# A chunk's contribution to the SSD state: one product of fp32 operands, or three products of split operands

## The chip, the cores and the metric

The kernel runs on one core of a Trainium2 chip. The metric is the device time of one execution in microseconds (us); runs are summed up by their median. Engines are named as in the profile: PE (TensorE, matrix products), PEld (its weight loads), DVE (VectorE), ACT (ScalarE), POOL (GpSimd) and SP (SyncE, which here only issues transfers). `L1535` is line 1535 of the kernel.

## The reference

One step of a decoder layer: a pooling branch beside a Mamba-2 SSD branch, merged by sigmoid gates, for a prompt of 1024 rows and 8 short samples. What matters here is the SSD of the prompt. The prompt is cut into 8 chunks of 128 rows, the 32 heads (64 wide each) form 4 groups of 8, and the heads of a group share B and C (128 wide). The state `h` is carried from chunk to chunk:

```
def step(h, inp):
    xq, dq, Bq, Cq = inp
    acs = jnp.cumsum(dq * Ag, axis=1)
    seg = acs[:, :, None] - acs[:, None, :]
    decay = jnp.exp(jnp.where(mask, seg, -jnp.inf))
    cb = jnp.einsum('bign,bjgn->bijg', Cq, Bq)
    att = cb[..., None] * decay * dq[:, None]
    y = jnp.einsum('bijge,bjgep->bigep', att, xq)
    y = y + jnp.einsum('bign,bige,bgepn->bigep', Cq, jnp.exp(acs), h)
    last = acs[:, -1]
    w_in = jnp.exp(last[:, None] - acs) * dq
    h = h * jnp.exp(last)[..., None, None] + jnp.einsum('bjgn,bjge,bjgep->bgepn', Bq, w_in, xq)
    return h, y
```

The last sum, over the rows `j` of a chunk, is the product that the change touches: B turned (rows by state, 128x128) against x weighted by `w_in` (rows by 8 heads of 64, 128x512), once per group and chunk, 32 times in all.

## The kernel before

All inputs are fp32. The large products are computed from split operands: a value is copied by ScalarE into a rounded high half (type fp32r), the rest (value less high half) is computed by VectorE or POOL as a low half, and three fp32r products, high·high, high·low and low·high, add up in PSUM (`gemm_`, `L359` to `L361`, here 12 products a block, that is three for each of four slices of 128 rows of the sum). Smaller products take fp32 operands as they are.

The work goes in stages: the first products and the modulation, the input projection (up to about 820 us, with the samples' SSD beside it), the chunk stage (about 820 to 1104 us), and the output products.

In the chunk stage, `chunk(g, c)` is a generator with one instance for each group `g` and chunk `c`, listed in `seq`, and each `yield` ends a step of it:

- loads of the decays (`dec`, L1492), of B and C (`bc`) and of x (`xb`, L1497), on SP's queue;
- the exponentials on ScalarE (`cE` L1501, `exps` L1201) behind a masking on POOL (`far` L1192);
- the transposes of x into the PSUM buffer `px` (L1510) and of B into `pbc` (L1512), and C·B (L1513) into the same buffer; ScalarE copies B turned to `bt` (L1515) and, for `c > 0`, C into `pbc` (L1517); VectorE makes `xd` (x by dt, L1521) and `xw` (x by `wdT`, L1523), and multiplies `dec` (L1528) and `cE` (L1530) by what stands in `pbc`;
- the state's product `pu` (L1535, PSUM pool `pc`, one buffer), the chunk's output `pi` (`inner`, L1213 and L1216), the new state `hn` (POOL L1541, VectorE L1543, or ScalarE L1539 for `c == 0`), and D·x added to `pi` in `xb` (L1548);
- `finish`: the gating by z (VectorE L1468), the split of the result (ScalarE L1470, POOL L1472), and sums of squares (ScalarE L1471, POOL L1473 to L1479);
- behind a group's last chunk, the state turned back (L1555), copied to a tile `fo` with the tag of x (L1557), and stored.

`px`, `pbc` and `pi` come from one PSUM pool, `ps`, of four buffers (`PB`). Blocks of the output products (`products`, from P_unit and S_unit) are woven in; they use the pool `mm` of three buffers (`PA`), and ScalarE (L1741) or VectorE (L1744, L1723) empties them. Their weights (`whi`, `wlo`, L459 and L460) are requested two units ahead (a unit is three blocks), with four buffers each. A loop over `i` sets the order; for the order of PE and SP what it traces is binding (`in_line(order)`), while DVE, ACT and POOL follow the order that the framework's scheduler gives them. In turn `i` stand the transposes of chunk `i + 1`, blocks, the products of chunk `i`, the loads of chunk `i + 3`, the exponentials of chunk `i + 2`, the finish of chunk `i`, a step of splitting w_o (`wo_splits`, ScalarE L1778, from `i > 12`), and blocks. 2.56 blocks come to a turn, so one or two lie between the products of a chunk and the next transposes.

Of the kernel before, what the change touches and what calls it, by code (L numbers as in the profile page):

```python
# [8 lines left out]
F32 = mybir.dt.float32  # L9
F32R = mybir.dt.float32r  # L10
AF = mybir.ActivationFunctionType
ALU = mybir.AluOpType
# [8 lines left out]
P = 128  # L21
# [25 lines left out]
def tile_pool_ssd_step(  # L47
# [9 lines left out]
    def nm(s):  # L57
        uid[0] += 1
        return f"{s}_{uid[0]}"
# [34 lines left out]
    def Y4(pool, dt=F32R):  # L94
        return pool.tile([P, 4, T], dt, tag="Y", name=nm("Y"), bufs=2)

    def PB():
        return psB.tile([P, 512], F32, tag="ps", name=nm("ps"))
# [4 lines left out]
    def PC():  # L103

        return psC.tile([P, 512], F32, tag="pc", name=nm("pc"))
# [6 lines left out]
    mm = nc.tensor.matmul  # L112
    act = nc.scalar.activation
    V = nc.vector
# [1069 lines left out]
    def decays(dec, g, c):  # L1184

        S = P if c < NC else NS
        load(dec, acs_d[c, 8 * g:8 * g + 8, :S].partition_broadcast(S))

    def far(dec, c):

        if c < NC:
            nc.gpsimd.affine_select(dec, dec, [[0, 8], [1, P]], ALU.is_ge, FAR, base=0, channel_multiplier=-1)  # L1192
        else:
            dS = dec.rearrange("p h (b i) -> p h b i", i=8)
            nc.gpsimd.affine_select(dS, dS, [[0, 8], [8, NB], [1, 8]], ALU.is_ge, FAR, base=0, channel_multiplier=-1)
            nc.gpsimd.affine_select(dS, dS, [[0, 8], [-8, NB], [0, 8]], ALU.is_ge, FAR, base=0, channel_multiplier=1)

    def exps(dec, g, c):
        S = P if c < NC else NS
        for h in range(8):  # L1200
            act(dec[:, h], dec[:, h], AF.Exp, bias=acT[:S, c, 8 * g + h:8 * g + h + 1], scale=-1.0)  # L1201
# [6 lines left out]
    def inner(xd, dec, S, state=None, cE=None):  # L1208
        pi = PB()
        for q in range(4):  # L1210
            o = [pi[64 * hh:64 * hh + 64, q * S:(q + 1) * S] for hh in range(2)]
            for hh in range(2):
                mm(o[hh], xd[:S, 2 * q + hh, :], dec[:S, 2 * q + hh], start=True, stop=state is None)  # L1213
            for hh in range(2 if state is not None else 0):
                h = 2 * q + hh
                mm(o[hh], state[:, h * 64:h * 64 + 64], cE[:, h], start=False, stop=True)  # L1216
        return pi[:, :4 * S].rearrange("p (q i) -> p q i", i=S)
# [245 lines left out]
    def ckt(shape, tag, bufs=2):  # L1463
        return (cl if tag in CKL else ca if tag in ("dec", "xb", "cE", "bc") else ck).tile(list(shape), F32, tag=tag, name=nm(tag), bufs=bufs)

    def finish(g, o, S, v, sz):

        V.tensor_tensor(v, v, sz, ALU.mult)  # L1468
        yhc = yh[g][:, :, o:o + S]
        act(yhc, v, AF.Copy)  # L1470
        act(sz, v, AF.Square)  # L1471
        nc.gpsimd.tensor_tensor(yl[g][:, :, o:o + S], v, yhc.bitcast(F32), ALU.subtract)  # L1472
        nc.gpsimd.tensor_tensor(sz[:, 0:2], sz[:, 0:2], sz[:, 2:4], ALU.add)  # L1473
        sa = sq_acc[:, o:o + S]
        if g == 0:
            nc.gpsimd.tensor_tensor(sa, sz[:, 0], sz[:, 1], ALU.add)
        else:
            nc.gpsimd.tensor_tensor(sz[:, 0], sz[:, 0], sz[:, 1], ALU.add)
            nc.gpsimd.tensor_tensor(sa, sa, sz[:, 0], ALU.add)  # L1479

    def sample_end(g):
        sz = ckt([P, 4, NS], "szs", 1)
        load(sz, z_d[g][:, :, SEQ:])
        v = ckt([P, 4, NS], "v", 1)
        load(v, ys_d[g])
        yield
        finish(g, SEQ, NS, v, sz)

    def chunk(g, c):
        o = c * P  # L1490
        dec = ckt([P, 8, P], "dec", 3)
        decays(dec, g, c)  # L1492
        bc = ckt([P, 2, P], "bc", 3)
        load(bc, xbc_d[g][:, 4:6, o:o + P])
        Bf, Cf = bc[:, 0], bc[:, 1]
        xb = ckt([P, 4, P], "xb", 5)
        load(xb, xbc_d[g][:, 0:4, o:o + P])  # L1497
        yield
        if c > 0:
            cE = ckt([P, 8, P], "cE")  # L1500
            act(cE, dec, AF.Exp, scale=-1.0)  # L1501
        if g > 0 or c > 0:
            far(dec, c)
            exps(dec, g, c)
            yield
        sz = ckt([P, 4, P], "sz", 3)
        load(sz, z_d[g][:, :, o:o + P])
        px = PB()
        for q in range(4):
            nc.tensor.transpose(px[:, q * P:(q + 1) * P], xb[:, q], ident)  # L1510
        pbc = PB()
        nc.tensor.transpose(pbc[:, :P], Bf, ident)  # L1512
        mm(pbc[:, P:2 * P], Bf, Cf, start=True, stop=True)  # L1513
        bt = ckt([P, P], "bt", 2)
        act(bt, pbc[:, :P], AF.Copy)  # L1515
        if c > 0:
            act(pbc[:, 2 * P:3 * P], Cf, AF.Copy)  # L1517
        pxv = px.rearrange("p (h d) -> p h d", d=64)
        heads = slice(8 * g, 8 * g + 8)
        xd = ckt([P, 8, 64], "xd", 2)  # L1520
        V.tensor_tensor(xd, pxv, dtT[:, c, heads].unsqueeze(2).to_broadcast([P, 8, 64]), ALU.mult)  # L1521
        xw = ckt([P, 8, 64], "xw", 1)
        V.tensor_tensor(xw, pxv, wdT[:, c, heads].unsqueeze(2).to_broadcast([P, 8, 64]), ALU.mult)  # L1523
        if g == c == 0:
            yield
            far(dec, c)
            exps(dec, g, c)
        V.tensor_tensor(dec, dec, pbc[:, P:2 * P].unsqueeze(1).to_broadcast([P, 8, P]), ALU.mult)  # L1528
        if c > 0:
            V.tensor_tensor(cE, cE, pbc[:, 2 * P:3 * P].unsqueeze(1).to_broadcast([P, 8, P]), ALU.mult)  # L1530
        yield
        if c == 0:
            yh[g], yl[g] = [Y4(hs if g % 2 else hp) for _ in range(2)]
        pu = PC()
        mm(pu, bt, xw.rearrange("p h d -> p (h d)"), start=True, stop=True)  # L1535
        pi = inner(xd, dec, P, *((hst[g], cE) if c > 0 else ()))
        hn = ckt([P, 512], "hst", 2)
        if c == 0:
            act(hn, pu, AF.Copy)  # L1539
        else:  # L1540
            nc.gpsimd.tensor_tensor(hn.rearrange("p (h d) -> p h d", d=64), hst[g].rearrange("p (h d) -> p h d", d=64),  # L1541
                                    Elb[:, c, heads].unsqueeze(2).to_broadcast([P, 8, 64]), ALU.mult)
            V.tensor_tensor(hn, hn, pu, ALU.add)  # L1543
        hst[g] = hn

        v = xb
        for q in range(4):
            V.scalar_tensor_tensor(v[:, q], v[:, q], Dv[:, 4 * g + q:4 * g + q + 1], pi[:, q], ALU.mult, ALU.add)  # L1548
        yield
        finish(g, o, P, v, sz)  # L1550
        if c == NC - 1:
            yield
            pt = PB()
            for q in range(4):
                nc.tensor.transpose(pt[:, q * P:(q + 1) * P], hn[:, q * P:(q + 1) * P], ident)  # L1555
            fo = ckt([P, 4, P], "xb", 5)
            act(fo, pt.rearrange("p (q n) -> p q n", n=P), AF.Copy)  # L1557
            store_(new_ssm_p[0, 0, 8 * g:8 * g + 8].rearrange("(q h) p n -> (h p) q n", h=2), fo)

# [125 lines left out]
    def to_chunks():  # L1685
        nonlocal right, ca
        right.__exit__(None, None, None)
        right = tc.tile_pool(name="ca", bufs=3, side="right", reuse_waits="tile")
        ca = right.__enter__()
        right_all.append(right)  # L1690
        seq.extend(chunk(g, c) for g in range(NG) for c in range(NC))
        next(seq[0])
    first_ws, first_g = {}, []
    ca = None
    seq = []
# [14 lines left out]
    ck = right.__enter__()  # L1710
# [78 lines left out]
    def products(t):  # L1789

        nonlocal made
        while made < RATE * t:
            next(pc_, None)
            made += 1
# [5 lines left out]
    for _ in range(FRONT - 1):  # L1800
        next(pc_)
    next(seq[0])
    next(seq[1])
    next(pc_)
    in_line(first_engines)
    order = tuple(mybir.EngineType[e] for e in ORDER)
    for i in range(len(seq)):
        if i + 1 < len(seq):
            next(seq[i + 1])
        products(i + 0.4)  # L1810
        if i > 0:
            next(seq[i - 1], None)
        next(seq[i], None)
        if i % NC == 2:
            ends = sample_end(i // NC)
            next(ends)
        if i + 3 < len(seq):
            next(seq[i + 3])
        if i + 2 < len(seq):
            next(seq[i + 2])  # L1820
        next(seq[i], None)
        if i % NC == 4:
            next(ends, None)
        if i > 12:
            next(wos, None)
        products(i + 1.0)
# [127 lines left out]
    for half in range(2):  # L1954
        c = slice(half * 512, half * 512 + 512)
# [102 lines left out]
```

## Time and profile before

| | |
|---|---|
| median of 3 runs | 1286.67 us (1284.23 to 1289.22) |
| profiled execution, its own time | 1286.55 us |
| its span, first to last instruction | 1284.8 us |
| mean granted clock of TensorE | 0.998 |
| PE busy in the span | 1256.1 us, 98% |
| DVE, ACT, POOL busy | 897.6 us (70%), 662.2 us (52%), 670.9 us (52%) |
| `L1535`, the product of the change | 64 records, 831.2 to 1101.8 us |

The profile shows one execution. A row of a group of instructions has the line, engine, operation, output and inputs by tile names, shapes and count, then the busy time and the mean duration, then the engine's idle time in front of these instructions with what ended it. The chain of waits goes back from the last instruction, at each step to what released it, or to the instruction ahead of it on its engine; a step's length is the time for which it held that path. The end of a product is modelled, and one product overlaps the next, so spacing is read from starts or from the chain, not from durations. An fp32 product of this kind leaves two records, one of split operands a single record.

### The profile page before, as it was taken

What the parts mean: (1) busy time and instruction counts of PE and PEld (TensorE: products, weight loads), DVE (VectorE), ACT (ScalarE), POOL (GpSimd) and SP (SyncE); (2) the same over time, 40 slices, a digit from 0 to 9 for tenths busy, and PEclk for the clock granted to TensorE, in tenths of its full rate; (3) what the DMA queues carried; (4) which work ended last, traced back from release to release, by engine and by line L of the source; (5) the groups of instructions that cost most, each with busy time, mean ns of one, the idle gap of its engine ahead of it and who ended that gap; (6) DMA issues with size and microseconds to landing.
All of it is one profiled execution on the core that took longest, in us unless ns stands there. A gap on an engine that the chain in (4) does not pass through costs nothing.

```text
span 1284.8 us, 26305 instructions
## 1 busy us (share of the span) xinstructions
PE 1256.1 (98%) x9739; PEld 1169.3 (91%) x9739; DVE 897.6 (70%) x1608; ACT 662.2 (52%) x1528; POOL 670.9 (52%) x563
## 2 busy tenths in 40 slices
PE   7999999999999999999999999999999999999997
PEld 6779999989999999999999999989888889999786
DVE  4686678965978688676676765587766877576443
ACT  4665347465556556454655554656675766202111
POOL 1007669678868878555444444355665867314000
PEclk9999999999999999999999999999999999999999
DMA  9736355465456544444556564999769898675631
GB/s 331 243 118 215 122 164 156 149 199 173 148 161 207 159 152 131 166 154 122 176 170 198 165 191 143 336 307 314 225 215 277 265 294 265 211 265 162 229 107 49
DMA packets 232769, 251.68 MB, mean 196 GB/s; under 512 B 29729, under 2 KB 176881, under 8 KB 232634
## 3 DMA queue, kind: packets, MB, share of 16 engines
q1 hardware_dynamic: 160544, 171.60, 42.9%
q10 hardware_dynamic: 72098, 78.41, 17.9%
q8 instruction: 77, 1.26, 0.4%
q14 instruction: 50, 0.41, 0.1%
HBM read 167.06 MB, written 83.01 MB: 195 GB/s over the span
## 4 chain that ended last, share of the span: by engine, by line
PE 63%; issue 7%; DMA 7%; POOL 4%; ACT 2%; DVE 2%; SPq 0%; ACTq 0%; POOLq 0%; DVEq 0%
PE ps L608 6%; PE ps L609 5%; PE ps L610 5%; PE mm L608 5%; PE mm L610 5%; PE mm L609 5%; PE mm L359 4%; PE mm L360 4%; PE mm L361 4%; PE ps L1213 3%; PE ps L2004 2%; PE ps L2006 2%; PE ps L2005 2%; PE pc L1535 2%; PE ps L1216 2%
## 5 line engine op out<-in xcount | busy, mean ns | idle before, releaser
L168 POOL TENSOR_TENSOR wlo<-rawA,whi 128x512 fp32r<-128x512 f32 x120 | 179.6, 1501 | 176.1 <-ACT whi L165 99.8
L168 POOL TENSOR_TENSOR wlo<-raw,whi 128x512 fp32r<-128x512 f32 x92 | 150.6, 1644 | 125.5 <-ACT whi L165 114.1
L359 PE MATMUL mm<-Y,whi 128*128 128x352 f32 (+1 forms) x480 | 163.5, 341 | 0.6 <-DVE G L1907 0.5
L360 PE MATMUL mm<-Y,whi 128*128 128x352 f32 (+1 forms) x480 | 157.4, 328 | 0.3 <-DVE Y L1573 0.3
L361 PE MATMUL mm<-Y,wlo 128*128 128x352 f32 (+1 forms) x480 | 156.8, 327 | 0.0
L608 PE MATMUL mm<-Y,whi 128*128 128x272 f32 x496 | 146.3, 295 | 0.6 <-DVE GA L624 0.5
L610 PE MATMUL mm<-Y,wlo 128*128 128x272 f32 x496 | 144.2, 291 | 2.2 <-POOL wlo L168 1.7
L608 PE MATMUL ps<-Y,whi 128*128 128x272 f32 x496 | 143.4, 289 | 2.5 <-ACT o L808 2.2
L609 PE MATMUL ps<-Y,whi 128*128 128x272 f32 x496 | 143.0, 288 | 0.0
L610 PE MATMUL ps<-Y,wlo 128*128 128x272 f32 x496 | 142.6, 287 | 0.0
L609 PE MATMUL mm<-Y,whi 128*128 128x272 f32 x496 | 142.6, 288 | 0.0
L1056 DVE SCALAR_TENSOR_TENSOR GA<-GA,cvT,GA 128x1112 f32<-128x1112 f32 x72 | 127.7, 1776 | 1.3 <-ACT GA L1053 1.3
L165 ACT ACTIVATE whi<-rawA 128x512 fp32r<-128x512 f32 x125 | 78.3, 627 | 89.7 <-PE ps L609 48.0
L165 ACT ACTIVATE whi<-raw 128x512 fp32r<-128x512 f32 x96 | 58.9, 627 | 104.6 <-DVE raw L554 48.7
L1201 ACT ACTIVATE dec<-dec,acT 128x128 f32<-128x128 f32 (+1 forms) x288 | 86.6, 383 | 23.2 <-POOL dec L1192 22.8
L610 PEld LDWEIGHTS mm<-Y,wlo 128*128 128x128 f32 x496 | 93.4, 188 | 3.8 <-POOL wlo L168 2.6
L359 PEld LDWEIGHTS mm<-Y,whi 128*128 128x128 f32 x480 | 90.2, 188 | 7.1 <-issue 4.8
L608 PEld LDWEIGHTS ps<-Y,whi 128*128 128x128 f32 x496 | 93.3, 188 | 3.1 <-ACT o L808 2.5
L608 PEld LDWEIGHTS mm<-Y,whi 128*128 128x128 f32 x496 | 93.3, 188 | 3.0 <-DVE GA L624 0.6
L609 PEld LDWEIGHTS mm<-Y,whi 128*128 128x128 f32 x496 | 93.4, 188 | 0.9
L610 PEld LDWEIGHTS ps<-Y,wlo 128*128 128x128 f32 x496 | 93.4, 188 | 0.0
L609 PEld LDWEIGHTS ps<-Y,whi 128*128 128x128 f32 x496 | 93.3, 188 | 0.0
(456 smaller groups left out, 3760.4 us busy)
## 6 DMA issues: line engine op xcount, KB each, us to landing
rawA<-in_w_in SPq DMA_DIRECT2D x46, 512.0 KB
dec<-acs_d SPq DMA_DIRECT2D x32, 512.0 KB
xbc<-GA ACTq DMA_DIRECT2D x24, 512.0 KB
rawA<-in_w_in SPq DMA_DIRECT2D x32, 256.0 KB
pw<-in_w_ssm_out ACTq DMA_DIRECT2D x32, 256.0 KB
ws<-ph ACTq DMA_DIRECT2D x32, 256.0 KB
ws<-pw SPq DMA_DIRECT2D x32, 256.0 KB
h<-in_state_ssm SPq DMA_DIRECT2D x32, 256.0 KB
```

What stands on the lines that cost most here:

```text
L165: ins = act(hi[:, :, :ncols], raw[:, :, :ncols], AF.Copy)
L168: (eng or nc.gpsimd).tensor_tensor(lo[:, :, :ncols], raw[:, :, :ncols], hi[:, :, :ncols].bitcast(F32), ALU.subtract)
L359: mm(ps[:, :n], a, rh[k][:, o:o + n], start=(k == 0), stop=False)
L360: mm(ps[:, :n], a, rl[k][:, o:o + n], start=False, stop=False)
L361: mm(ps[:, :n], b, rh[k][:, o:o + n], start=False, stop=(k == nk - 1))
L608: mm(p, hi, ah, start=(k == 0), stop=False)
L609: mm(p, hi, al, start=False, stop=False)
L610: mm(p, lo, ah, start=False, stop=(k == 3))
L1056: V.scalar_tensor_tensor(d[:, :n], rp[:, k:k + n], cvT[:, 24 * k + mc:24 * k + mc + 1], d[:, :n], ALU.mult, ALU.add)
L1201: act(dec[:, h], dec[:, h], AF.Exp, bias=acT[:S, c, 8 * g + h:8 * g + h + 1], scale=-1.0)
L1213: mm(o[hh], xd[:S, 2 * q + hh, :], dec[:S, 2 * q + hh], start=True, stop=state is None)
L1216: mm(o[hh], state[:, h * 64:h * 64 + 64], cE[:, h], start=False, stop=True)
```

## The change

The product `pu` is made from split operands. x is weighted in place in PSUM (the output of L1523 is `pxv` itself), and a new step splits weighted x into `xwh` and `xwl` (512 wide) and B turned into `bth` and `btl` (128 wide): the high halves by ScalarE, the low ones by VectorE, both out of PSUM. Three products then add up in `pu`. The tile `xw` and the two buffers of `bt` give way to four tiles of one buffer each, and the tile tag of x has four buffers instead of five. The loop gets one call more in each turn, so that the split of chunk `i + 1` is traced behind the products of chunk `i`; the opening gets one for chunk 0.

```
-        xb = ckt([P, 4, P], "xb", 5)
+        xb = ckt([P, 4, P], "xb", 4)
...
         pbc = PB()
         nc.tensor.transpose(pbc[:, :P], Bf, ident)
         mm(pbc[:, P:2 * P], Bf, Cf, start=True, stop=True)
-        bt = ckt([P, P], "bt", 2)
-        act(bt, pbc[:, :P], AF.Copy)
         if c > 0:
             act(pbc[:, 2 * P:3 * P], Cf, AF.Copy)
...
         V.tensor_tensor(xd, pxv, dtT[:, c, heads].unsqueeze(2).to_broadcast([P, 8, 64]), ALU.mult)
-        xw = ckt([P, 8, 64], "xw", 1)
-        V.tensor_tensor(xw, pxv, wdT[:, c, heads].unsqueeze(2).to_broadcast([P, 8, 64]), ALU.mult)
+        V.tensor_tensor(pxv, pxv, wdT[:, c, heads].unsqueeze(2).to_broadcast([P, 8, 64]), ALU.mult)
...
         yield
+
+        bth, btl = (ck.tile([P, P], F32R, tag=t, name=nm(t), bufs=1) for t in ("bt", "btl"))
+        xwh, xwl = (ck.tile([P, 512], F32R, tag=t, name=nm(t), bufs=1) for t in ("xw", "xwl"))
+        act(xwh, px, AF.Copy)
+        act(bth, pbc[:, :P], AF.Copy)
+        V.tensor_tensor(xwl, px, xwh.bitcast(F32), ALU.subtract)
+        V.tensor_tensor(btl, pbc[:, :P], bth.bitcast(F32), ALU.subtract)
+        yield
         if c == 0:
             yh[g], yl[g] = [Y4(hs if g % 2 else hp) for _ in range(2)]
         pu = PC()
-        mm(pu, bt, xw.rearrange("p h d -> p (h d)"), start=True, stop=True)
+        mm(pu, bth, xwh, start=True, stop=False)
+        mm(pu, btl, xwh, start=False, stop=False)
+        mm(pu, bth, xwl, start=False, stop=True)
...
-            fo = ckt([P, 4, P], "xb", 5)
+            fo = ckt([P, 4, P], "xb", 4)
...
     next(seq[0])
+    next(seq[0])
     next(seq[1])
...
         next(seq[i], None)
+        if i + 1 < len(seq):
+            next(seq[i + 1])
         if i % NC == 2:
```

## The prediction

> **What bounds the kernel now.** I read the page's first lines, then the busy time of each engine by stage, then TensorE's own list of waits.
>
> ```profile
> span 1284.8 us, 26305 instructions
> PE 1256.1 (98%) x9739; PEld 1169.3 (91%) x9739; DVE 897.6 (70%) x1608; ACT 662.2 (52%) x1528; POOL 670.9 (52%) x563
> ```
>
> ```profile
> 831.00:898.00 67.00, 67.00 (x545) 59.33 (x544) 54.55 (x98) 35.91 (x95) 34.05 (x39) 1.00 0.95 303
> ...
> 831.00:1102.00 271.00, 269.92 (x2165) 239.50 (x2163) 208.25 (x362) 166.89 (x432) 174.66 (x201) 1.00 0.85 266
> ```
>
> ```profile
> 1102.00:1200.00 98.00, 97.02 (x579) 91.17 (x579) 58.45 (x108) 13.28 (x24) 26.34 (x17) 1.00 0.65 224
> 1200.00:1270.00 70.00, 70.00 (x304) 55.80 (x303) 28.48 (x37) 11.56 (x24) 0.00 (x0) 1.00 0.32 115
> ```
>
> ```profile
> PE ps L1512 <- DVE cE L1530: 1.1, 1, 1.1
> ```
>
> The columns of the stage rows are length, then busy time of PE, PEld, DVE, ACT and POOL, the granted clock, the DMA share and GB/s. The changed lines run in the chunk stage, 831 to 1102 us. TensorE is busy there for 269.92 of 271 us at a clock of 1.00, and the 1.1 us that it lacks are one wait, for VectorE. The stages behind it are full too (97.02 of 98, 70.00 of 70), so what TensorE saves in the chunks reaches the end. VectorE is next: 208.25 us, 77%, and 54.55 of 67 (81%) in the first eight chunks. The question is thus how much TensorE time goes, and whether VectorE or ScalarE give it back.
>
> **The change, part by part.**
>
> *Three products instead of one (saves).* The chain of waits gives each step the time for which it held the path. First a chunk, then the last stage, where products of 512 columns follow one another; then the count.
>
> ```profile
> 909.13 0.86 PE pc L1535 x2
> 909.99 0.37 PE ps L1213 x4
> 910.36 0.22 PE ps L1216 x4
> ```
>
> ```profile
> 1213.08 0.23 PE ps L2005
> 1213.31 0.24 PE ps L2006
> ```
>
> ```profile
> L1535 PE MATMUL pc<-xw,bt x64: 590/591/595, 831.2 to 1101.8; 128*128 128x512 f32 x64
> ```
>
> The product of full fp32 operands (two records each, 64 records for 32 chunks) holds the path 0.86 us. A 512-column product of split operands holds it 0.23 or 0.24 us, so three take 0.69 to 0.72; I take 0.69, since 0.23 is the commoner value in that stretch. Saved: 0.86 - 0.69 = 0.17 us a chunk, 32 x 0.17 = 5.4 us (4.5 by the upper price). The first four `L1213` cost 0.37 instead of the 0.22 of the four `L1216` behind them; that 0.15 is the step from whole-array weights to 64-column ones. I leave it in, because a split product ahead of narrow weights pays as well:
>
> ```profile
> 631.56 0.29 PE L609 MATMUL ps<-Y,whi 128*128 128x272 f32 x1
> 631.69 0.29 PE L610 MATMUL ps<-Y,wlo 128*128 128x272 f32 x1
> 631.91 0.42 PE L1317 MATMUL pc<-hT,cz 128*32 128x128 f32 x8
> ```
>
> Starts are 0.13 us apart between split products and 0.22 before the narrow one, 0.09 more. Bounds for this term: 0 and a gain of 0.15 - 0.09 = 0.06 a chunk (1.9 us); I take 0.
>
> *Splitting B and the weighted x (adds to VectorE and ScalarE).*
>
> ```profile
> L1528 DVE TENSOR_TENSOR dec<-dec,ps 128x1024 f32<-128x1024 f32 x31 | 37.8, 1219 | 32.2 <-ACT ps L1517 22.6 <-ACT bt L1515 5.3 <-POOL Y L1472 2.5
> ...
> L1523 DVE TENSOR_TENSOR xw<-ps,wdT 128x512 f32<-128x512 f32 x31 | 21.2, 684 | 10.9 <-PE pc L1535 10.9
> ```
>
> ```profile
> L1286 DVE TENSOR_TENSOR bt<-ps,bt 32x128 fp32r<-32x128 f32 x8 | 2.3, 284 | 1.9 <-ACT bt L1285 1.8
> ```
>
> ```profile
> L1515 ACT ACTIVATE bt<-ps 128x128 f32<-128x128 f32 x30 | 7.8, 259 | 4.6 <-PE ps L1513 4.6
> ...
> L1539 ACT ACTIVATE hst<-pc 128x512 f32<-128x512 f32 x4 | 2.4, 589 | 2.8 <-PE pc L1535 1.4 <-PE mm L361 1.4
> ```
>
> VectorE gets two subtractions: `xwl`, 512 wide with one operand in PSUM, 0.68 us as `L1523`, and `btl`, 128 wide, 0.28 us as `L1286`, the same operation on fewer partitions. That is 0.96 a chunk, 30.7 us in all. The weighting stays, 0.68 us, but writes into PSUM. No VectorE row shows a full-size write there. By its reads I keep 0.68; the bounds are 0.59 (ScalarE on the same tile, `L1539`) and 1.22 (`L1528`, twice as wide), so -2.9 to +17 us of VectorE time. It no longer waits for the product before it to release `xw`: 10.9 us of waiting go. ScalarE gets the copy `xwh`, 0.59 (18.9 us); `bth` replaces `bt` at 0.26.
>
> Sums: VectorE 208.25 + 30.7 = 239 us of the 266 left, 90%; in the first eight chunks 54.55 + 7.7 = 62.3 of 65.6, 95%. ScalarE 166.89 + 18.9 = 186, 70%. Neither exceeds TensorE, and the results aren't needed until the next turn, some 8 us later. So I cost this work at nothing where only throughput counts. The cover is thin for VectorE: 5% in the first quarter.
>
> *The hand-over between engines (adds a wait).* A chunk uses three of the four PSUM buffers `ps`: x turned (`px`), B turned with C·B and C (`pbc`), and the output (`pi`). Now `px` is free after VectorE's weighting, and `pbc` after `L1530`. Afterwards `px` goes VectorE, ScalarE (`xwh`), VectorE (`xwl`), and `pbc` goes ScalarE, VectorE, ScalarE (`bth`), VectorE (`btl`). TensorE's next transposes (`L1510`, `L1512`) stand behind these buffers, and everything on TensorE stands behind them. `L1528` above waited 22.6 us for `L1517`, though it reads other columns of the buffer than `L1517` writes: two engines take turns on a buffer. [...]
>
> The one place where the old wait reaches TensorE:
>
> ```profile
> 963.73 4.72 DMA dec<-acs_d
> ...
> 991.19 0.27 ACT ps L1517
> ...
> 991.54 1.22 DVE dec L1528
> ...
> 994.15 0.30 PE ps L1512
> ```
>
> ```profile
> 969.15 1.02 PE L1535 MATMUL pc<-xw,bt 128*128 128x512 f32 x2
> ...
> 977.94 1.02 PE L1535 MATMUL pc<-xw,bt 128*128 128x512 f32 x2
> ...
> 987.60 1.02 PE L1535 MATMUL pc<-xw,bt 128*128 128x512 f32 x2
> ```
>
> From 963.73 to 994.15 the path runs through loads, stores and ScalarE, not through products. Three chunk products lie in this stretch, so 3 x 0.17 = 0.5 us of lead is lost to waiting. And `L1512` waits for the last read of a buffer, which will be `btl` instead of `L1530`: `bth` 0.26 and `btl` 0.28, each behind a hand-over of 0.08 (`L1517` ends at 991.46, `L1528` starts at 991.54), 0.7 us. Bounds: 0, where another buffer comes free first, and 1.4, with `xwl` between. I take 0.7.
>
> *The extra step.* The split is issued one turn ahead, behind the chunk's products; it moves no transfer on SP's or POOL's queue and no product on TensorE. On ScalarE `cE` and the exponentials of a later chunk queue behind it, with a turn to spare. Cost 0.
>
> *Four buffers of x.*
>
> ```profile
> 903.17 0.41 SPq L1497 DMA_DIRECT2D xb<-xbc  x1
> ...
> 905.79 1.28 POOL L1472 TENSOR_TENSOR Y<-xb,Y 128x512 fp32r<-128x512 f32 x1
> ...
> 911.71 0.32 SPq L1187 DMA_DIRECT2D dec<-acs_d  x1
> ...
> 912.60 0.42 SPq L1497 DMA_DIRECT2D xb<-xbc  x1
> ```
>
> The second load here, of x three chunks ahead, now takes the buffer of the chunk before, last read by POOL until 907.07; it is issued at 912.60, held back by TensorE's release of `dec` (911.71) anyway. Only behind a group's end, three times, does the state's output `fo` occupy a buffer, and then the load may have to wait for the `L1472` of its own turn: the first load here stands at 903.17, and the `L1472` behind it ends at 907.07, so at most 3.9 us. Behind it on SP stand weights that are fetched two units ahead, at least six blocks of 12 x 0.16 us, 11.5 us. Cost 0; if the cover were gone, up to 3.9 us three times.
>
> **Sum** against the profiled execution's own 1286.55 us (span 1284.8 and 1.75 around it; the median shown is 1286.67, 0.12 above): 1286.55 - 5.4 + 0.5 + 0.7 = 1282.35, which I round to 1282.4, -0.3%.
>
> **The rivals.**
>
> *Buffers come back too late (slower).* In 15 of 30 turns only one block of products lies between a chunk's products and the next transposes, about 2 us from the first `L359` to `L1510` instead of 4. The first and the last of them on the chain of waits, and one turn in detail:
>
> ```profile
> 833.25 0.38 PE mm L359
> 835.54 0.44 PE ps L1510 x4
> ...
> 1087.64 0.36 PE mm L359
> 1089.76 0.44 PE ps L1510 x4
> ```
>
> ```profile
> 911.94 1.12 DVE L1548 SCALAR_TENSOR_TENSOR xb<-xb,Dv,ps 128x128 f32<-128x128 f32 x4 [0.47 <-PE ps L1216]
> ...
> 913.10 1.61 DVE L1468 TENSOR_TENSOR xb<-xb,sz 128x512 f32<-128x512 f32 x1
> ...
> 914.29 0.27 PE L1512 MATMUL ps<-ident,bc 128*128 128x128 f32 x1
> ```
>
> If VectorE runs `xwl` and `btl` behind both of these, `btl` ends at 914.71 + 0.68 + 0.28 = 915.7, and `L1512`, due at 914.1, waits 1.6 us; behind `L1548` alone it ends at 914.0 and nothing waits. With `L1468` at 0.68, what 512 elements cost in `L1523`, it is 0.6 us. Fifteen times 0.6 to 1.6 is 9 to 24 us on 1286.55 - 5.4: 1290 to 1305. It decides once the halves end more than 2.2 us after the chunk's last product. Against it: `pi` is free after `L1548`, and the waits of `L1528` (32.2 us) and `L1523` (10.9 us) are room for the halves ahead of it. For it: VectorE at 95%, or at 96% over the stage if the write into PSUM costs its 1.22. Chance 0.15.
>
> *No gain.* The lead is eaten by what TensorE doesn't pace, transfers (share 0.85 to 0.95) or a VectorE at 95%: 1286.5. Against it: TensorE's waits in this stage name no transfer. Chance 0.17.
>
> *Cheaper products.* Three products that share weights could follow closer than 0.23 us; the shortest row is 0.16, of 352 columns. 32 x (0.86 - 0.48) = 12.2 us would go: 1274.4. Against it: row after row of 512 columns at 0.23. Chance 0.06. [...]
>
> **How the numbers follow.** The sum's case has 0.62 and its own range of 1280 (all of 5.4, and the 1.1 us wait gone) to 1285. The runs of this kernel spread over 1284.2 to 1289.2, so 0.5% (6.4 us) is about what can be told. Range: 1279 leaves out the cheap products, 1293 takes in no gain and the mild end of late buffers. Faster by over 0.5% (under 1280.2): cheap products and the low edge of the sum's case, 0.12. Slower (over 1293.1): most of the late buffers, 0.13. Same 0.75.
>
> **What would show it.** Right: the chain holds about 0.69 for three `pc` products and still about 0.37 for the first `L1213`; PE's busy time in the chunk stage falls by about 5 us and its waits there stay under 3; VectorE's rises by about 31. Wrong: waits of `L1510` or `L1512` for `btl`, `xwl` or `xwh` in many turns; `pc` products at 0.29 each, which is no gain; VectorE's weighting near 1.2 us; blocks (`L359`) waiting for evictions.

## The result, and the profile after

The changed kernel takes 1299.28 us (median of 6 runs, 1296.86 to 1300.25), the kernel before 1287.44 beside it: a ratio of 1.0091, 95% interval 1.0078 to 1.0105. It is slower by 0.9%, some 12 us. The profiled execution took 1296.86 us, 10.31 more than the one shown of before, and is the fastest of the six.

Lines have moved in the changed kernel: the split is `L1532` to `L1535`, the three products `L1540` to `L1542`, the copy of C `L1515`, D·x `L1555`. Of w_o's pieces, `L1790` is the load (`L1783` before), `L1785` ScalarE's copy of the high half (`L1778`), `L1787` POOL's low half (`L1780`), and `L1782` the store of a finished low half, on SP's queue too.

The page's first lines, and the busy time by stage (length, then PE, PEld, DVE, ACT and POOL, granted clock, DMA share, GB/s):

```profile
span 1295.1 us, 26494 instructions
PE 1254.1 (97%) x9771; PEld 1175.8 (91%) x9771; DVE 924.9 (71%) x1672; ACT 681.0 (53%) x1562; POOL 670.9 (52%) x563
```

```profile
831.00:898.00 67.00, 64.94 (x545) 59.83 (x541) 57.90 (x111) 42.98 (x113) 32.89 (x37) 1.00 0.91 294
831.00:1112.00 281.00, 268.06 (x2188) 246.95 (x2184) 232.83 (x422) 184.98 (x474) 173.88 (x201) 0.99 0.82 257
```

TensorE did less: 1254.1 us busy, not 1256.1. But it now idles in the chunk stage: 281.00 - 268.06 = 12.9 us, against 1.1 before. From the first to the last state product the stage takes 281.7 us, not 270.2. The chain of waits shows the cheaper products:

```profile
908.91 0.23 PE pc L1540
909.14 0.23 PE pc L1541
909.38 0.23 PE pc L1542
909.61 0.37 PE ps L1213 x4
909.98 0.22 PE ps L1216 x4
```

TensorE's waits in the stage (engine, output, line, what ended the wait; total, times, longest; "issue" means that the profile shows nothing that it waited for):

```profile
PE ps L1512 <- issue: 8.1, 3, 3.3
PE ps L1512 <- PE ps L1510: 3.4, 5, 0.9
PE ps L1510 <- DMA xb<-xbc: 0.7, 1, 0.7
PE ps L1512 <- DVE xb L1555: 0.6, 1, 0.6
```

They add up to 12.8 us, 12.1 of it at the transpose of B (`L1512`). SP stands at the load of x for 38.5 us in all; before it was 2.3, the longest 1.4. The largest of these waits:

```profile
SPq L1497 <- POOL Y L1472: 16.2, 8, 11.6
SPq L1497 <- DMA out<-xb: 13.0, 3, 6.9
SPq L1497 <- ACT sz L1471: 6.8, 4, 2.8
```

One of TensorE's two long waits in detail, from SP's, ScalarE's, VectorE's and TensorE's rows (start, length, and in brackets the idle time ahead):

```profile
1047.22 0.43 SPq L1494 DMA_DIRECT2D bc<-xbc  x1
1053.27 0.37 SPq L1497 DMA_DIRECT2D xb<-xbc  x1
1054.30 0.43 SPq L1790 DMA_DIRECT2D pw<-in_w_o  x1
...
1059.49 0.63 ACT L1785 ACTIVATE ph<-pw 128x512 fp32r<-128x512 f32 x1 [8.29 <-DMA pw<-in_w_o]
...
1060.58 0.60 ACT L1532 ACTIVATE xw<-ps 128x512 fp32r<-128x512 f32 x1 [0.46 <-ACT ph L1785]
...
1061.21 0.69 DVE L1534 TENSOR_TENSOR xwl<-ps,xw 128x512 fp32r<-128x512 f32 x1 [5.46 <-ACT xw L1532]
1061.81 0.28 DVE L1535 TENSOR_TENSOR btl<-ps,bt 128x128 fp32r<-128x128 f32 x1
...
1062.00 0.30 PE L1512 MATMUL ps<-ident,bc 128*128 128x128 f32 x1 [3.13 <-issue]
```

SP has B and C at 1047.22 and gets to x only at 1053.27; the piece of w_o behind it (`L1790`) goes out at 1054.30. ScalarE stands 8.29 us at `L1785` for it. The split of x (`L1532`) stands behind `L1785` on ScalarE; VectorE stands 5.46 us for that. `xwl` is the last reader of `px`, and TensorE goes on at 1062.00, 0.10 us behind its end (1061.21 + 0.69).

The other long wait, 3.31 us before 994.84, ends 0.10 us behind `xwl` too (994.06 + 0.68), but is less plain. There the split was not what VectorE stood for: VectorE had waited 5.74 us for ScalarE's copy of C (`L1515`) and then worked without a gap from 990.73. ScalarE had stood 4.39 us at `L1785` some 6 us before that copy; that the one led to the other is not shown for this wait by itself. The third wait that is put down to issue, 1.68 us before 1032.55, ends 0.10 us behind D·x (`L1555`), the last reader of `pi`.

At both long waits the granted clock falls:

```profile
994.00:998.00 4.00, 3.16 (x13) 0.57 0.96 232
1062.00:1066.00 4.00, 4.00 (x16) 0.57 0.28 103
```

In the second stretch (length, busy time, granted clock) that is 4 x 0.43 = 1.7 us lost while TensorE counts as busy. In the first the clock was at half 0.7 us before the wait ended, so that 1.4 us are lost there. The stage's account: 12.8 - 1.1 = 11.7 us more of waits, 3.1 of half clock, and 3.3 less of everything else (the remainder) make the 11.5 us. The remainder is 1.6 us short of the 4.9 that the products save by themselves (below); where that goes is open.

### The profile page after: what moved, and what is told of

Its sections match the earlier page's. It is cut to its first block, busy times and chain, and to the rows that moved or that the text cites. A ratio compares the mean times of both kernels' runs of the same rounds, so it can differ in the third digit from the quotient of the medians.

```text
span 1295.1 us, 26494 instructions
## 1 busy us (share of the span) xinstructions
PE 1254.1 (97%) x9771; PEld 1175.8 (91%) x9771; DVE 924.9 (71%) x1672; ACT 681.0 (53%) x1562; POOL 670.9 (52%) x563
## 4 chain that ended last, share of the span: by engine, by line
PE 76%; issue 9%; DMA 4%; DVE 4%; POOL 4%; ACT 3%; ACTq 0%; SPq 0%; POOLq 0%; DVEq 0%
PE ps L608 7%; PE ps L609 7%; PE mm L608 7%; PE ps L610 7%; PE mm L610 7%; PE mm L609 7%; PE mm L359 4%; PE mm L361 4%; PE mm L360 4%; PE ps L1213 3%; PE ps L2016 2%; PE ps L2015 2%; PE ps L2014 2%; PE ps L1216 2%; PE ps L233 2%
## 5 line engine op out<-in xcount | busy, mean ns | idle before, releaser
L1201 ACT ACTIVATE dec<-dec,acT 128x128 f32<-128x128 f32 (+1 forms) x288 | 86.4, 383 | 19.5 <-POOL dec L1192 18.8
```

## The experiments

Theory A: the time is lost because SP stands at `L1497` for one of only four buffers of x, and what queues behind it is late. Theory B: the split itself holds PSUM buffers too long, whatever the buffers of x. Each kernel is compared with the kernel before on its own chip (medians of 1284.7 to 1287.4 there). "Stage" is the distance from the first to the last state product in the profiled execution, taken between like records; "waits" are TensorE's from 820 to 1125 us. Both are one execution each; that of the changed kernel with half tiles is the slowest of its five, 1300.63 us. In "before, w_o behind the stage" the 1.2 us of waits all lie behind the last state product.

| kernel | median us | ratio to before (95%) | stage | waits |
|---|---|---|---|---|
| before | 1287.44 | 1 | 270.2 | 1.1 |
| changed | 1299.28 | 1.0091 (1.0078, 1.0105) | 281.7 | 12.8 |
| changed, `fo` elsewhere | 1290.54 | 1.0037 (1.0013, 1.0061) | 274.9 | 8.9 |
| before, 4 buffers of x | 1289.95 | 1.0033 (1.0010, 1.0055) | 273.9 | 4.6 |
| before, three products alone | 1284.05 | 0.9981 (0.9959, 1.0003) | 265.3 | 1.5 |
| changed, w_o halves on POOL | 1298.63 | 1.0093 (1.0062, 1.0123) | 282.9 | 13.7 |
| changed, x loaded later | 1288.61 | 1.0023 (1.0010, 1.0036) | 273.3 | 7.5 |
| before, x loaded later | 1289.84 | 1.0031 (1.0019, 1.0044) | 273.9 | 2.8 |
| before, w_o behind the stage | 1321.53 | 1.0270 (1.0248, 1.0292) | 268.9 | 1.2 |
| changed, w_o behind, 5 buffers | 1316.69 | 1.0234 (1.0215, 1.0254) | 265.8 | 1.5 |
| changed, w_o behind, 4 buffers | 1316.60 | 1.0232 (1.0218, 1.0245) | 267.3 | 2.7 |
| before, half tiles of w_o | 1294.52 | 1.0054 (1.0042, 1.0066) | 278.8 | 6.5 |
| changed, half tiles, 5 buffers | 1295.88 | 1.0067 (1.0054, 1.0080) | 283.0 | 13.6 |
| the same, split a step earlier | 1296.21 | 1.0071 (1.0059, 1.0084) | 280.5 | 10.7 |
| changed, w_o behind the split on ScalarE | 1287.24 | 1.0024 (1.0010, 1.0038) | 270.4 | 5.2 |
| the same, x loaded later | 1290.78 | 1.0048 (1.0029, 1.0066) | 273.9 | 6.5 |

### The state's output moved off the tag of x

```
-            fo = ckt([P, 4, P], "xb", 4)
+            fo = ckt([P, 4, P], "hst", 2)
```

> The changed kernel, but the turned state fo takes a buffer of the tag hst, so that the four buffers of x belong to x alone. Theory A (buffers of x): fo and its store occupy one of four, SP stands at the load of x (L1497), the load of w_o behind it comes late, ScalarE waits for it in L1785 with xwh behind, and the PSUM buffer that L1512 needs comes late. Then the two waits of 3.3 and 3.1 us and the 0.7 us at L1510 go, and with them the two stretches of half clock (3.4 us each, 1.7 us lost in each): 1299.3 - 7.1 - 3.4 = about 1289. Theory B (hand-over alone): the PSUM buffers are held too long in every turn, whatever SP does: 1297 to 1300.

1290.54 us: about 0.5% comes back. Both long waits are gone (the longest that is put down to issue is 1.1 us), and the granted clock of the whole execution is 0.997 (0.996 in the changed kernel, 0.998 before); in their place there is one wait of 2.3 us for x itself (`L1510`). SP still stands at `L1497` for the finish (`L1472`), 14.3 us in 6. ScalarE still stood at `L1785` once for 6.2 us with the split behind it, and TensorE waited only 0.5 us there. So the buffer of x that `fo` takes starts the worst of it. The tag `hst` is no free place either: POOL, which makes the next state there, stood 9.1 us for the store of `fo`.

### Four buffers of x in the old kernel

```
-        xb = ckt([P, 4, P], "xb", 5)
+        xb = ckt([P, 4, P], "xb", 4)
```

and the same for `fo`.

> The kernel before with four buffers of x instead of five and nothing else. Theory A: SP stands at L1497 behind each group's end as in the changed kernel (36 us in all there), and ScalarE waits longer for w_o, but nothing that TensorE needs soon stands behind ScalarE's wait, so at most a few us: 1287.4 to 1291. Theory B: no change, 1287.4.

1289.95 us, ratio 1.0033: the buffer that I costed at nothing is worth 0.33%, some 4 us, with nothing else changed. SP stands there as in the changed kernel:

```profile
SPq L1497 <- DMA out<-xb: 15.0, 3, 5.6
SPq L1497 <- POOL Y L1472: 13.4, 7, 8.9
```

Yet TensorE waits 4.6 us here and 12.8 in the changed kernel. Nearly the same stand at `L1497` (36.0 us in all, there 38.5) costs the changed kernel more.

### The three products alone

The operands are written as fp32r by the instructions that made them, and the product is done three times with the same operands: the low halves are left out, and so are the split, its hand-over and the loss of a buffer.

```
-        mm(pu, bt, xw.rearrange("p h d -> p (h d)"), start=True, stop=True)
+        for n in range(3):
+            mm(pu, bt, xw.rearrange("p h d -> p (h d)"), start=n == 0, stop=n == 2)
```

> The kernel before, with bt and xw written as fp32r by the instructions that write them anyway, and three products of the same two operands in place of one fp32 product (the low halves are left out, so the state's term is three times too large). It is TensorE's part of the change alone. Both theories: 32 x 0.17 us less, 1287.4 - 5.4 = 1282, less about 0.5 us that is lost where the path is not TensorE's. If split products cost more among fp32 ones than in the last stage, 1285 to 1287.

1284.05 us, 0.9981 (0.9959 to 1.0003): the forecast of 1282 isn't reached, and total and interval don't tell it from no change. But the stage is 4.9 us shorter (265.3 against 270.2), and the chain has

```profile
908.39 0.70 PE pc L1536 x3
```

0.70 for three products, where one of fp32 held it 0.86. The profiled execution as a whole is only 2.5 us shorter than that of before: behind the stage, from 1098 to 1200 us, its mean granted clock is 0.98, an estimated 2.0 us (102 x 0.02) that is lost there; in the profile of before it is 1.00 over the same stretch. The prediction took for granted that what TensorE saves in the chunks reaches the end; here a part of it didn't.

### w_o's high half on POOL

```
-                act(hi, raws[n - 1], AF.Copy)
+                nc.gpsimd.tensor_copy(hi, raws[n - 1])
```

> The changed kernel, with the high half of w_o copied by POOL instead of ScalarE (L1785). Theory A: SP still stands at L1497 and the loads of w_o still come late, but ScalarE no longer waits for them ahead of xwh; the waits of L1512 at 991 and 1059 us shrink to under 1 us: about 1289 to 1291. Theory B: 1297 to 1300.

1298.63 us, no help. ScalarE no longer stands for w_o, but POOL does:

```profile
POOL ph L1785 <- DMA pw<-in_w_o: 25.2, 8, 8.8
```

```profile
PE ps L1510 <- DMA xb<-xbc: 6.2, 2, 4.8
PE ps L1512 <- issue: 3.9, 2, 2.1
```

The finish (`L1472`), which frees x's buffer, is on POOL behind it; SP stands longer and x itself is late. On either engine, what stood behind a late piece of w_o was late.

### Room for a fifth buffer, taken from w_o: four kernels

Five buffers of x don't fit beside the tiles of the split. With two buffers of `pw` instead of three they do:

```
-                raws[n] = ck.tile([P, 512], F32, tag="pw", name=nm("pw"), bufs=3)
+                raws[n] = ck.tile([P, 512], F32, tag="pw", name=nm("pw"), bufs=2)
```

The changed kernel so, with `xb` at 5:

> The changed kernel with its five buffers of x back; the room comes from the tiles that w_o is loaded to (pw, two buffers instead of three). Theory A (buffers of x): SP no longer stands at L1497, the lead of the loads is as in the kernel before, and what is left is TensorE's saving of about 5 us: 0.996 to 0.999 of the kernel before. Theory B (the halves hold PSUM buffers and VectorE in every turn): the waits of L1512 that the kernel with fo in hst still had (about 6 us) stay: 1.000 to 1.004.

Its control, the kernel before with two buffers of `pw`:

> The kernel before with two tiles pw instead of three, to price that loan alone. Both theories: 1.000, at most 1.002, since TensorE does not wait for w_o in this stage; if it does cost, e7 and e9 are to be read against it.

The changed kernel so, with the split in the step of the weighting (one `yield` and its two calls less):

> As e7_xb5_pw2, but the split is traced in the step that weights x, ahead of the chunk products of the turn and without the extra step, so that the scheduler ranks it ahead of the state, of the output's sum and of the finish. Theory B: the PSUM buffers come back earlier, L1512 waits less than in e7, 0.996 to 0.998. Theory A: no difference from e7 beyond 0.1%. If ScalarE stands at xwh for the product before to release the tile, it is slower than e7 instead: 1.002 or more.

The changed kernel so, without `xwl` and `btl`, the product of the high halves done three times (the low halves are left out):

> As e7_xb5_pw2, without the low halves (xwl and btl are left out, and the product of the high halves is made three times, so the state's term is wrong). VectorE has 0.96 us a turn less to do and a hand-over less. Theory B: the waits of L1512 go, 0.996 to 0.998, by about 3 to 6 us below e7. Theory A: as e7, within 0.1%.

They took 1322.72, 1321.87, 1320.71 and 1320.84 us, ratios to before 1.0284 (1.0262, 1.0306), 1.0277 (1.0253, 1.0302), 1.0263 (1.0240, 1.0285) and 1.0276 (1.0255, 1.0296): nothing among them can be told apart. One buffer of `pw` less cost the control 36 us by itself, where 0.2% at most had been forecast. SP stands there at the load of w_o for the store of a piece before:

```profile
SPq L1783 <- DMA wo<-pw: 96.2, 14, 8.1
```

As a test of A against B this failed: it put a larger stall of the same kind into both. The last of the four says one thing more. With no low halves, TensorE's waits name ScalarE's copy of x:

```profile
PE ps L1512 <- ACT xw L1532: 15.1, 6, 4.3
```

So the waits behind `L1532` don't need VectorE's two subtractions.

### x loaded a turn later

The load of x gets a step of its own at the start of a turn, for the chunk two ahead instead of three, so that four buffers are enough by count; `fo` goes to `hst`. The same edit in both kernels:

```
+        if 8 * g + c > 2:
+            yield
         xb = ckt([P, 4, P], "xb", 4)
...
     for i in range(len(seq)):
+        if 0 < i < len(seq) - 2:
+            next(seq[i + 2])
```

The changed kernel:

> The changed kernel with its four buffers of x; the load of x is moved one turn later (a step of its own at the start of a turn, for the chunk two ahead instead of three), and `fo` takes a tile of the tag `hst`. Theory A (the time is lost because SP stands at L1497 for one of four buffers, and x and w_o behind it come late): SP no longer waits at the load of x, PE's waits at L1512 fall from 12.1 us to under 3, and the time falls from 1299 to 1281 to 1285, under the kernel before. Theory B (the split step itself holds PE up): PE still waits 5 us or more at L1512, and the time stays at 1289 to 1292, as where `fo` alone was moved. A third way: x comes too late by its own load, and PE waits at L1510 for it, 1 to 3 us a time.

The kernel before:

> The kernel before with four buffers of x, the load of x moved one turn later, and `fo` in the tag `hst`. Theory A: with the load moved the fifth buffer is not needed: 1284 to 1287, against 1290 with four buffers and the load as it was. The difference to the changed kernel with the same move is then the products alone, 3 to 5 us in favour of the split ones. Theory B: the split kernel with the same move is slower than this one by 3 us or more.

1288.61 and 1289.84 us; the one over the other, from their 12 runs each, is 0.9990 (0.9975 to 1.0005). Both expectations of A missed: neither gets back to before, and SP still stands at the load (10.0 and 10.7 us for `L1472`), which POOL finishes late. Two new costs came with the edit: TensorE waits for x itself (3.7 us in 2, 2.6 in 2), and POOL for the store of `fo` (16.4 and 14.5 us). But under equal terms the split is no slower than the old product, nor is it the 3 to 5 us faster that A had forecast: B alone isn't the 12 us.

### The splitting of w_o out of the stage

```
-        if i > 12:
-            next(wos, None)
...
+    wz_cm = tc.tile_pool(name="wz", bufs=2, side="right", reuse_waits="tile")
+    wz = wz_cm.__enter__()
+    for _ in wos:
+        pass
+    wz_cm.__exit__(None, None, None)
```

The kernel before so:

> The kernel before with the splitting of w_o taken out of the chunk stage and done behind it, in a pool of its own. The total rises by what the splitting then takes in the open, an estimate of 20 to 50 us; the number to read is the stage, first to last product of L1535: 266 to 270 us by both theories (270.1 before). It is the control of the next kernel.

The changed kernel so, with five buffers of x:

> The changed kernel with the splitting of w_o behind the chunk stage in the same way, and five buffers of x, for which there is then room. Theory A: the stage is 3 to 5 us shorter than in the control, and so is the total (ratio to the control's 0.996 to 0.998). Theory B: the stage is not shorter than the control's, and PE waits 4 us or more at L1512 with SP free.

And with its own four:

> The changed kernel with the splitting of w_o behind the chunk stage, and the four buffers of x of the change (with five it took 1316.7). If four buffers cost only through the splitting of w_o that stands behind x on SP: 1316 to 1318, and PE's waits at L1512 stay at 1 to 3 us. If SP standing for a buffer of x costs by itself, through x and the weights of the blocks: 1319 to 1323, with waits of SP at L1497 of 10 us or more and of PE at L1510 or L1512 of 4 us or more.

1321.53, 1316.69 and 1316.60 us. The change over its control is 0.9966 (0.9943 to 0.9989, from four runs each): 4.8 us by the medians, in the direction and of the size that the sum gave; of it the stage shows 3.1 us (268.9 against 265.8), and the interval is wide. And four buffers of x or five makes no difference that can be told there, although SP still stands at `L1497`, for 21.2 us in all:

```profile
SPq L1497 <- POOL Y L1472: 8.8, 3, 7.2
SPq L1497 <- DMA out<-xb: 5.5, 3, 4.1
```

So with w_o's pieces out of the stage this much of SP's standing costs nothing that can be told; with them in it, x itself came late too in two kernels (2.3 us with `fo` elsewhere, 6.2 with w_o's halves on POOL). What is left of TensorE's waits with five buffers, both in the first eight chunks:

```profile
PE ps L1512 <- PE ps L1510: 0.9, 1, 0.9
PE ps L1512 <- DVE xb L1555: 0.6, 1, 0.6
```

Both end about 0.1 us behind the end of D·x (`L1555`), which reads `pi`, and not behind a half.

### Half tiles of w_o

w_o in pieces of 256 columns, two in a turn, four buffers of `pw` and two of `ph`; that leaves room for five buffers of x with w_o in the stage.

```
-                raws[n] = ck.tile([P, 512], F32, tag="pw", name=nm("pw"), bufs=3)
+                raws[n] = ck.tile([P, 256], F32, tag="pw", name=nm("pw"), bufs=4)
...
             next(wos, None)
+            next(wos, None)
```

The changed kernel so:

> The changed kernel with five buffers of x. The room comes from the tiles of w_o: halves of 256 columns, two of them in a turn, four buffers of `pw` and two of `ph`. Theory A (buffers of x): SP no longer waits at L1497, PE's waits at L1512 are 1 to 3 us, and the time is 1280 to 1284, under the kernel before. Theory B (the hand-over through the split step): 1287 or more. Against both: the halves double the transfers and the fixed costs of ScalarE and POOL for w_o; what that costs the control shows.

The kernel before so:

> The kernel before with w_o split in the same half tiles, its five buffers of x unchanged. The control of the kernel above: 1285 to 1288 if half tiles cost nothing. Theory A: the changed kernel with halves is 3 to 5 us faster than this one. Theory B: it is not faster.

The changed kernel so, with the split in the step of the weighting:

> The changed kernel with five buffers of x and half tiles of w_o as above, and the split traced in the step of the weighting, so that it stands ahead of the products of the chunk before in the order of ScalarE and VectorE, and the two PSUM buffers of x and B come back sooner. If what is left of PE's waits at L1512 in the first eight chunks (about 1.5 us) comes from the split's place: 1 to 2 us faster than with the step of its own. If the earlier split delays what VectorE has to do for the products: no change, or 1 to 3 us slower.

1295.88, 1294.52 and 1296.21 us. A's forecast fell, and B's (no faster than its control) held: SP waits at `L1497` for 1.3 us at the longest, and still TensorE waits as in the changed kernel, and ScalarE for pieces of w_o, whose loads now stand for the stores of high halves (`L1790`, 7.8 us in 7):

```profile
PE ps L1512 <- issue: 9.9, 4, 4.2
PE ps L1512 <- PE ps L1510: 2.8, 5, 0.8
```

```profile
ACT ph L1785 <- DMA pw<-in_w_o: 12.2, 11, 2.4
ACT ph L1785 <- issue: 8.2, 2, 4.5
```

So a lack of x buffers is one cause of late pieces, not the only one. That these late pieces are what makes TensorE wait was not tested with half tiles: the edit of ScalarE's order that follows was made with whole tiles only. Half tiles cost the kernel before 7.5 us against the run beside it. The earlier split changed nothing that can be told.

### ScalarE's order alone

```
-                act(hi, raws[n - 1], AF.Copy)
+                with behind(mybir.EngineType.Activation):
+                    act(hi, raws[n - 1], AF.Copy)
```

The copy of w_o is issued behind the square of the finish (`L1471`), and so no longer ahead of the split of x.

> The changed kernel with one edit: ScalarE's copy of w_o (L1785) may be issued only behind the last instruction that was traced for ScalarE before it (the square of the finish, L1471), so that it stands behind the split of x (L1532) in ScalarE's order and no longer ahead of it. If PE's long waits at L1512 come through ScalarE: the waits put down to issue (8.1 us in 3) fall to under 2, the time falls from 1299 to 1290 to 1294, and what is left is SP's standing at L1497. If the link is x itself or VectorE: no change, 1297 to 1301, and the waits are as they were.

1287.24 us, ratio 1.0024 where the changed kernel had 1.0091: one instruction's place on ScalarE takes back 0.67%, about 8.6 us, more than expected. No stretch of half clock is left in the stage: the granted clock is 1.00 in each of four windows from 831 to 1105 us. TensorE's largest waits:

```profile
PE ps L1512 <- PE ps L1510: 1.9, 4, 0.9
PE ps L1512 <- issue: 1.5, 1, 1.5
```

SP still stands (27.4 us at `L1497`). In the turn that was shown in detail above it does so from the load of B and C at 1044.39 to that of x at 1049.53, but the split now comes first, and the copy of w_o (here `L1786`) behind it without a wait:

```profile
1044.39 0.43 SPq L1494 DMA_DIRECT2D bc<-xbc  x1
1049.53 0.37 SPq L1497 DMA_DIRECT2D xb<-xbc  x1
```

```profile
1051.39 0.60 ACT L1532 ACTIVATE xw<-ps 128x512 fp32r<-128x512 f32 x1 [2.29 <-PE pc L1541]
...
1056.87 0.61 ACT L1786 ACTIVATE ph<-pw 128x512 fp32r<-128x512 f32 x1
```

In the whole stage ScalarE now waits for no piece of w_o; in the changed kernel it was 16.2 us in 6.

With x loaded later and `fo` in `hst` besides:

> The same edit, with the load of x one turn later and `fo` in the tag `hst` (1288.6 without the edit). If ScalarE's order and SP's standing are the two links: 1282 to 1286, and PE waits 3 us or less in the chunk stage. If not: 1287 to 1291.

1290.78 us, a miss: worse than either edit alone. POOL stood 13.5 us for the store of `fo` (the longest 8.6) and TensorE 2.1 us for x; that the combination falls behind for these two reasons was not tested.

No complete kernel of these beats the kernel before. The changed kernel with one link cut, on ScalarE (1.0024) or on SP (1.0023), comes nearest.

## Why the prediction was wrong

**The three products: right.** 0.23 each on the chain, 0.37 for the first `L1213` as before. The term of 5.4 us shows as 4.9 in the stage with the products alone; in the changed kernel's account 3.3 are left of it.

**The work on VectorE and ScalarE: right.** Weighting in place in PSUM costs what it cost into SBUF, the value that I kept between the bounds:

```profile
L1520 DVE TENSOR_TENSOR ps<-ps,wdT 128x512 f32<-128x512 f32 x32 | 21.9, 686 | 0.0
L1534 DVE TENSOR_TENSOR xwl<-ps,xw 128x512 fp32r<-128x512 f32 x32 | 21.9, 683 | 10.2 <-ACT xw L1532 10.2
```

```profile
L1535 DVE TENSOR_TENSOR btl<-ps,bt 128x128 fp32r<-128x128 f32 x32 | 9.0, 281 | 0.0
```

VectorE rose by 27.3 us (897.6 to 924.9), ScalarE by 18.8. In the first eight chunks VectorE was busy for 57.90 of 67 us, 86%, not for 95%.

**The hand-over: the right place, the wrong reader, low in size.** The 0.7 us was 1.5 with w_o out of the way, all of it in the first eight chunks. But these two waits end behind D·x, and the two long waits of the changed kernel ended behind `xwl`; of the waits followed here none ended behind `btl`, which the prediction had named. The rival of late PSUM buffers, 0.6 to 1.6 us in fifteen turns, names the right place (`L1512`) and its range holds the time measured, but not by its cause: with w_o away, TensorE waits at `L1512` twice in 32 turns, not fifteen times.

**Four buffers of x, "Cost 0": the step that failed.** I saw that the load behind `fo` may wait for the finish of its own turn and put it at 3.9 us; it was up to 11.6. Three times it stood for the store of `fo` as well, 13.0 us, which I had not counted. Two more things were missed. The wait feeds itself: the finish runs on POOL, in line behind POOL's part of w_o (`L1787`), which waits for ScalarE's (`L1785`), which waits for the piece that SP hasn't issued. POOL's waits there, of before and of after:

```profile
POOL pw L1780 <- ACT ph L1778: 8.7, 7, 2.8
```

```profile
POOL pw L1787 <- ACT ph L1785: 28.8, 11, 7.3
```

And as cover I named only the weights of the blocks behind `L1497`, not the next queue entry but one, `L1790`. The profile of before had a sign of this path. There ScalarE stood 2.42 us for a piece of w_o, with the copy of C (`L1517`, 991.19) directly behind it, and behind that copy stands TensorE's only wait in the stage, the 1.1 us before 994.15:

```profile
990.65 0.63 ACT L1778 ACTIVATE ph<-pw 128x512 fp32r<-128x512 f32 x1 [2.42 <-DMA pw<-in_w_o]
```

I had read the chain of waits there, which names a load of `szs` ahead of `L1517`, a tile that `L1517` doesn't read, and not ScalarE's own row ahead of it.

**The extra step, "Cost 0": wrong with it.** I counted what queues behind the split on ScalarE (`cE`, the exponentials), and not what the split queues behind. It put on ScalarE an instruction that TensorE's next transposes depend on, and `L1785`, which waits for a transfer, stood ahead of it. That place is shown by experiment: with only it changed, 8.6 of the 12 us come back; with w_o elsewhere, four buffers cost nothing that can be told and the change gains 4.8 us.

**The sum.** 1282.4 would have needed both costs at nothing. With w_o out of the way the gain is there, but only against a control that takes 1321.53 us. That the kernel with ScalarE's order mended is still 0.24% above before, not below, is put down by its profile to 5.2 us of waits; which of SP's remaining stands causes each is open.

## What to carry to other kernels

When a step of a hot path is given to another engine, list what that engine's queue holds ahead of it, and above all each instruction there that waits for a transfer: here the split of x stood on ScalarE behind `L1785`, which waited 8.29 us for a piece of w_o, and VectorE stood 5.46 us for the split. When a buffer is taken away, follow the queue behind the load that may now stand to its end, past the first entry that is well covered. And a test that makes room by taking a buffer elsewhere needs its control first; here the loan cost 36 us and hid what was to be seen.

## What the runs showed of the hardware

Some waits of TensorE cost more than their length. In the changed kernel, at those of 3.31 and 3.13 us, the granted clock was at half (0.50) for about 3.4 us, worked out from its mean in each microsecond (0.56, 0.50, 0.50 and 0.73 from 994 us on; 0.70, 0.50, 0.50 and 0.60 from 1062 us on). That cost 1.4 and 1.7 us more. In the last kernel above (order and later load) half clock followed a wait of 2.1 us. The wait, and behind it length, busy time and granted clock:

```profile
PE ps L1512 <- DMA xb<-xbc: 2.1, 1, 2.1
```

```profile
1075.00:1076.00 1.00, 1.00 (x7) 0.57 1.06 386
1076.00:1077.00 1.00, 1.00 (x5) 0.50 1.08 412
1077.00:1078.00 1.00, 1.00 (x5) 0.50 1.04 381
```

The length of a wait doesn't decide it. With x loaded later in the kernel before, the longest wait was 2.0 us, and the granted clock was 0.98 from 1034 to 1105 us, the window that it lies in. Waits of up to 2.5 us (changed, x loaded later) and 2.9 us (before, 4 buffers of x) left it at 1.00 in each of four windows from 831 to 1105 us. And in the products alone it was 0.98 from 1098 to 1200 us, where TensorE was busy for 100.87 us; before, with 101.02 us, it was 1.00 there. What decides is not shown here.

VectorE writing 128x512 into PSUM in place took 0.686 us, into SBUF (`L1523` of before) 0.684.
